# Weights 128 bytes away from the operands that stream past them

## The chip, the cores and the metric

The kernel runs on one core of a Trainium2 chip. The metric is device time in microseconds of one execution; where several runs are given, the median. Everything said of the hardware comes from the profile of one execution, taken by the hardware profiler: for each engine when an instruction started, how long it took and what it waited for. PE is TensorE (matmuls), PEld its loading of weights, DVE is VectorE, ACT ScalarE, POOL GpSimd; SP issues most of the DMA transfers.

## The reference

Two layers of an encoder block on 512 tokens of width 1024, all in float32:

```python
for l in range(DEPTH):
    x = x + 0.5 * swiglu_ffn(rmsnorm(x, ffn1_norm[l]), ffn1_w_in[l], ffn1_w_out[l])
    h = rmsnorm(x, mix_norm[l])
    u_rwkv, u_gla, u_xa, u_gate = split_cols(h @ w_in[l], (RWKV_COLS, GLA_COLS, XA_WIDTH, GATE_COLS))
    y_rwkv, v_first = rwkv7_mixer(u_rwkv, v_first, ...)
    y_gla = gla_mixer(u_gla, ...)
    y_xa = memory_attention(u_xa, rmsnorm(mem, mem_norm[l]), xa_w_kv[l])
    branches = jnp.stack([y_rwkv, y_gla, y_xa], axis=2)
    merged = jnp.einsum('bsjc,jcd,bsjd->bsd', branches, w_branch[l], jax.nn.sigmoid(gates))
    x = x + merged @ w_out[l]
    x = x + 0.5 * swiglu_ffn(rmsnorm(x, ffn2_norm[l]), ffn2_w_in[l], ffn2_w_out[l])
return rmsnorm(x, final_norm)
```

`swiglu_ffn` is `(silu(gate) * up) @ w_out` with a hidden width of 2816. Most of the work is matrix products with weights, in the four FFNs and in the projection `w_in` and the branches of the mixer.

## The kernel before

**Products in two halves.** A float32 operand is split into a rounded `hi` (ACT) and the rest `lo` (DVE, source minus `hi`), and a product is three matmuls: hi with hi, hi with lo, lo with hi. Activations are laid out with features on the partitions. In most products the weights are the stationary operand, 128 columns at a time, and the activations stream past them, 256 or 512 columns per matmul. In the row of a matmul, `ps_b<-xhi,hi` names the output, the streamed operand and the weights, in this order.

**Seven products instead of eight.** `seven` computes a product of 2x2 blocks by Winograd's scheme: seven parts, each a chain of 3n matmuls of 128x256 in `part` (n is 4, or 3 in the last block of the hidden width). The left factors are sums of quarters of the weights, made on DVE or by adding DMA transfers. They come as pieces, which `piece` splits into `hi` and `lo`:

- a *wide* piece holds the weights of two parts (`raw.shape[1] == 2`, 128x1024): `a` for the parts with `b11` and `n1`, `q` for `n2` and `b21`. Its halves stand in pool `wp` under the tags `whi` and `wlo`.
- a *narrow* piece holds those of one part (128x512): `e` twice, for `t3` and `b22`, and `d` for `t4`. Its halves stand in the pool of the stage (`ffn`, or `mg` in the mixer) under the tags `fhi` and `flo`, two buffers of each.

So a product has four parts on wide pieces and three on narrow ones. The right factors are made once: by `blocks_in` in pool `keep` (`xhi`, `xlo`, `n12`, `t3`) for the first FFN weight, and in the pool of the stage (`mh`, `ml`) for the second FFN weight and for the mixer's `w_out`. Tile `n12` shows in rows as `n`, `t3` as `t`.

**Where the work lies.** Each of the four FFNs has 22 hidden tiles. The first four are plain products of three matmuls of 128x512 on all of x (`whole`), the other 18 go through `seven`. After each block of 8, 8 and 6 hidden tiles, four calls of `seven` apply that block's rows of the second weight. In the mixer the projections are plain products with weights in `wp` (`wide`), 128x512 each, between many small float32 matmuls of the recurrences; the memory's keys are products of 128x256; `w_out` goes through `seven` four times per layer.

**Memory.** Pools are entered in the order `const`, `keep`, `wp`, `nrm`, and then those of the stage; tiles follow each other within a pool. A tile's start is rounded up to 32 bytes, so that each of the two `rt` buffers in `nrm`, 16 bytes long, takes 32; all other tiles of `keep`, `wp` and `nrm` are multiples of 256 bytes. `const` ends so that `keep` starts at 128 modulo 256. Hence the tiles of `keep`, `wp` and the `sq` tiles of `nrm` start at 128 modulo 256, those of `ffn` at 192.

**Order.** Every operation is first recorded; `plan` then simulates the engines with durations that depend on shapes only and issues each engine's queue in the order that the simulation finds. A tile's buffer is free for its next tile when all users of the old one are done (`gone`).

Of the kernel before, what the change touches and what calls it, by code (L numbers as in the profile page):

```python
# [11 lines left out]
F32 = mybir.dt.float32  # L12
F32R = mybir.dt.float32r
# [6 lines left out]
P = 128  # L20
T = 512
# [7 lines left out]
HALVES = slice(0, H), slice(H, T)  # L29
NWHOLE = [[4, 4], [4, 4]]  # L30
NWARM = 12
NQ = 5
EPS = 1e-6
LN_EPS = 64e-5
# [63 lines left out]
class Tile:  # L98
    def __init__(self, pool, shape, dt, name, tag, bufs):
        self.pool, self.shape, self.dt, self.name, self.tag, self.bufs = pool, shape, dt, name, tag, bufs  # L100
        self.real, self.users, self.writes, self.reads, self.runs = None, [], [], [], ([], [])
        self.before, self.gone, self.free = (), None, False
# [491 lines left out]
class Net:  # L594
    def __init__(self, ctx, tc, I):
        self.nc, self.I = Recorder(tc), I
        self.const = self.pool("const", 1)
        self.keep = self.pool("keep", 1)
        self.wp = self.pool("wp", 2)
        self.nrm = self.pool("nrm", 1)  # L600
        self.psb = self.pool("psb", 3, space=PSUM)
        self.pss = self.pool("pss", 1, space=PSUM)
        self.psy = self.pool("psy", 1, space=PSUM)
        self.dram = self.pool("dram", 1, space=bass.MemoryType.DRAM)
# [24 lines left out]
    def setup(self):  # L629
        nc, I = self.nc, self.I  # L630
        self.pars = [self.const.tile([P, NPAR], F32, name=f"par{l}", tag=f"par{l}") for l in range(L)]
        self.par = self.pars[0]
        nc.scalar.dma_start(out=self.par, in_=I["par"][0])
        self.one = self.const.tile([P, 1], F32, name="one", tag="one")
        nc.vector.memset(self.one, 1.0)
        ps = self.psy.tile([P, T], F32, name="ps_y", tag="y", free=True)
        for _ in range(NWARM):
            nc.tensor.matmul(ps[:, :P], self.one.to_broadcast([P, P]), self.one.to_broadcast([P, P]), start=True, stop=True)
        self.turn = 0
        self.xs = self.keep.tile([P, KD, T], F32, name="x", tag="x")  # L640
        self.x = [self.xs[:, k, :] for k in range(KD)]
        for k in range(KD):
            nc.sync.dma_start(out=self.x[k], in_=I["x"][k * P:(k + 1) * P, :])
        self.cst = self.const.tile([P, P], F32, name="cst", tag="cst")
        nc.sync.dma_start(out=self.cst, in_=I["cst"][:, :P])
        for l in range(1, L):
            nc.sync.dma_start(out=self.pars[l], in_=I["par"][l])
        self.eps = self.const.tile([P, 2], F32, name="eps", tag="eps")
        nc.vector.memset(self.eps[:, 0:1], EPS)
        nc.vector.memset(self.eps[:, 1:2], LN_EPS)  # L650

        self.sums, self.par7 = {}, False
        self.yd = self.dram.tile([3, P, T], F32, name="yd", tag="yd")
        self.yx = self.dram.tile([4, P, T], F32, name="yx", tag="yx")
        self.xd = self.dram.tile([KD, P, T], F32, name="xd", tag="xd")
        self.vd = [self.dram.tile([4, P, T], F32, name=f"vd{l}", tag=f"vd{l}") for l in range(L)]
# [127 lines left out]
    def raw_in(self, pool, norm):  # L784

        hi, lo = (pool.tile([P, 7, T], F32R, name="xr" + c, tag=f"m01{c}", bufs=1) for c in "hl")
        r = pool.tile([P, 2, T], F32R, name="xr", tag="q", bufs=NQ)
        xs = [(hi[:, k, :], lo[:, k, :]) for k in range(7)] + [(r[:, 0], r[:, 1])]
# [44 lines left out]

    def piece(self, pool, raw):

        p, tags = (self.wp, ("whi", "wlo")) if raw.shape[1] == 2 else (pool, ("fhi", "flo"))
        hi, lo = (p.tile(list(raw.shape), F32R, name=t[1:], tag=t, bufs=2) for t in tags)
        self.split(hi, lo, raw)
        return [(hi[:, c, :], lo[:, c, :]) for c in range(raw.shape[1])]

# [56 lines left out]
    def seven(self, pool, src, n, ops, evict, clear=False):  # L897
# [7 lines left out]
        def begin():  # L905
# [3 lines left out]
            nc.gpsimd.dma_start(out=a[:, 1], in_=w[:, 3], accum_op=ALU.add)  # L909
            q = ring("q", NQ)  # L910
            nc.sync.dma_start(out=q[:, 1], in_=w[:, 2])
            e = ring("q", NQ)
            nc.sync.dma_start(out=e[:, 0], in_=w[:, 1])
# [871 lines left out]
    def mem_norm(self, pool):  # L1785

        nc, I = self.nc, self.I
        mt = [pool.tile([P, 4, NMEM], F32, name="m", tag="q", bufs=NQ) for _ in range(2)]
        mt = [t[:, k, :] for t in mt for k in range(4)]
# [118 lines left out]
```

## Time and profile before

| | |
|---|---|
| median of 3 runs | 2533.76 us (2532.69 to 2534.31) |
| the profiled execution's own time | 2534.68 us |
| its span, first to last instruction | 2532.7 us |
| granted clock of TensorE | 0.999 |
| ACT busy | 1466.9 us, 58% of the span |
| POOL busy | 241.2 us, 10% |
| DMA | 358.02 MB, 141 GB/s in the mean |

The busy time of an engine is the union of its instructions. Matmuls overlap one another in their pipeline, so a row's duration is longer than the time from one start to the next; the latter, called pace below, is what a chain of matmuls costs. In a group's row stand the count, the busy time, the mean duration of one in ns, and the idle time before them with what ended it.

### The profile page before, as it was taken

To read this page: it belongs to the slowest core of one execution; us is meant where nothing else is said; L and a number is where in the kernel's file an instruction comes from. 1 tells how busy PE (TensorE), PEld (TensorE's weight loads), DVE (VectorE), ACT (ScalarE), POOL (GpSimd) and SP (SyncE) were. 2 spreads that over 40 slices of the span, in tenths; PEclk is the share of its full clock that TensorE was granted. 3 is DMA by queue.
4 is the path that set the end of the run, shared out by engine and by line. 5 is a ranking of instruction groups with operands and counts; after the bars stand their busy time and mean duration, and the time that the engine had idled before them with its cause. 6 is when DMAs were issued, how large, how long until landed. Compare 5 with 4: busy or idle time off the path is not lost.

```text
span 2532.7 us, 47197 instructions
## 1 busy us (share of the span) xinstructions
PE 2506.4 (99%) x17636; PEld 2270.3 (90%) x17636; DVE 2100.5 (83%) x4218; ACT 1466.9 (58%) x2660; POOL 241.2 (10%) x362
## 2 busy tenths in 40 slices
PE   9999999999999999999999999999999999999998
PEld 8999988888788799999989999887887888899998
DVE  8988885778888689888899888866888877898878
ACT  6665666564544456565665656664745444565655
POOL 1111100000000001111112111000000000011110
PEclk9999999999999999999999999999999999999999
DMA  7777762422222456877558777523222225468774
GB/s 199 194 197 189 165 190 76 125 73 69 70 83 74 141 159 150 204 186 184 143 143 203 187 184 170 176 88 101 84 72 88 67 77 171 134 162 205 188 180 105
DMA packets 163668, 358.02 MB, mean 141 GB/s; under 512 B 18256, under 2 KB 38160, under 8 KB 163440
## 3 DMA queue, kind: packets, MB, share of 16 engines
q1 hardware_dynamic: 125344, 288.87, 37.8%
q0 software_dynamic: 36864, 65.03, 16.2%
q8 instruction: 139, 2.28, 0.4%
q10 hardware_dynamic: 1232, 1.11, 0.1%
q14 instruction: 89, 0.73, 0.1%
HBM read 342.88 MB, written 12.06 MB: 140 GB/s over the span
## 4 chain that ended last, share of the span: by engine, by line
PE 85%; DVE 8%; DMA 3%; ACT 2%; issue 2%; SPq 0%; DVEq 0%; ACTq 0%; POOLq 0%
PE ps_b L316 40%; PE ps_i L316 25%; PE ps_f L316 10%; PE ps_c L316 9%; PE ps_y L316 1%; DVE wlo L316 1%; DVE lo L316 1%; DVE x L316 1%; DMA q<-in_ffn_out_dram 1%; ACT whi L316 1%; DMA wraw<-in_w_out_dram 0%; DVE ml L316 0%; DMA wraw<-in_ffn_in_dram 0%; ACT hi L316 0%; DMA q<-in_ffn_in_dram 0%
## 5 line engine op out<-in xcount | busy, mean ns | idle before, releaser
L316 ACT ACTIVATE hi<-q 128x512 fp32r<-128x512 f32 (+3 forms) x384 | 288.9, 756 | 204.8 <-PE ps_i L316 69.6
L316 DVE TENSOR_TENSOR lo<-q,hi 128x512 fp32r<-128x512 f32 (+3 forms) x384 | 321.6, 840 | 43.5 <-ACT hi L316 43.1
L316 PE MATMUL ps_b<-xhi,whi 128*128 128x512 f32 (+1 forms) x880 | 353.7, 402 | 0.2 <-DVE rk_r L316 0.2
L316 PE MATMUL ps_b<-xlo,whi 128*128 128x512 f32 (+1 forms) x880 | 352.9, 401 | 0.1
L316 PE MATMUL ps_b<-xhi,wlo 128*128 128x512 f32 x864 | 347.2, 402 | 0.6 <-DVE wlo L316 0.6
L316 DVE TENSOR_TENSOR wlo<-wraw,whi 128x1024 fp32r<-128x1024 f32 (+1 forms) x172 | 183.7, 1069 | 75.2 <-ACT whi L316 71.0
L316 ACT ACTIVATE whi<-wraw 128x1024 fp32r<-128x1024 f32 (+1 forms) x174 | 161.7, 929 | 130.0 <-PE ps_b L316 100.1
L316 DVE TENSOR_TENSOR lo<-wraw,hi 128x1024 fp32r<-128x1024 f32 (+2 forms) x162 | 191.5, 1182 | 48.5 <-ACT hi L316 46.5
L316 ACT ACTIVATE hi<-wraw 128x1024 fp32r<-128x1024 f32 (+2 forms) x162 | 166.3, 1026 | 106.1 <-PE ps_i L316 41.0
L316 PEld LDWEIGHTS ps_b<-xlo,whi 128*128 128x128 f32 (+1 forms) x880 | 164.1, 187 | 35.6 <-DVE xlo L316 2.5
L316 PEld LDWEIGHTS ps_b<-xhi,whi 128*128 128x128 f32 (+1 forms) x880 | 164.4, 187 | 33.6 <-issue 1.2
L316 PEld LDWEIGHTS ps_b<-xhi,wlo 128*128 128x128 f32 x864 | 162.7, 188 | 32.9 <-DVE wlo L316 2.4
L316 PE MATMUL ps_i<-mh,hi 128*128 128x256 f32 x628 | 157.1, 283 | 4.3 <-ACT hi L316 2.6
L316 PE MATMUL ps_i<-ml,hi 128*128 128x256 f32 x624 | 154.8, 281 | 0.0
L316 PE MATMUL ps_b<-xlo,hi 128*128 128x256 f32 x576 | 144.3, 283 | 0.0
L316 PE MATMUL ps_b<-xhi,hi 128*128 128x256 f32 x576 | 144.3, 283 | 0.0
L316 PEld LDWEIGHTS ps_i<-mh,hi 128*128 128x128 f32 x628 | 119.1, 190 | 5.9 <-ACT hi L316 3.2
L316 PEld LDWEIGHTS ps_i<-ml,hi 128*128 128x128 f32 x624 | 118.1, 190 | 0.0
L316 PEld LDWEIGHTS ps_b<-xhi,hi 128*128 128x128 f32 x576 | 110.5, 192 | 0.2
L316 PEld LDWEIGHTS ps_b<-xlo,hi 128*128 128x128 f32 x576 | 110.4, 192 | 0.2
L316 DVE TENSOR_TENSOR q<-q 128x512 f32<-128x512 f32 (+1 forms) x128 | 85.5, 668 | 22.9 <-DMA q<-in_ffn_in_dram 19.0
L316 ACT ACT_TABLE_LOAD x71 | 91.1, 1283 | 18.9 <-DVE gc L316 10.8
(416 smaller groups left out, 7021.4 us busy)
## 6 DMA issues: line engine op xcount, KB each, us to landing
wraw<-in_w_main_dram SPq DMA_DIRECT2D x108, 512.0 KB, 3.6
wraw<-in_ffn_in_dram SPq DMA_DIRECT2D x102, 512.0 KB, 4.6
q<-in_ffn_in_dram SPq DMA_DIRECT2D x144, 256.0 KB, 4.5
d<-in_ffn_in_dram SPq DMA_DIRECT2D x72, 256.0 KB, 4.2
q<-in_ffn_in_dram POOLq DMA_DIRECT2D x72, 256.0 KB, 6.0
wraw<-in_ffn_in_dram POOLq DMA_DIRECT2D x72, 256.0 KB, 5.2
wraw<-in_ffn_out_dram SPq DMA_DIRECT2D x32, 512.0 KB, 4.4
q<-in_ffn_out_dram SPq DMA_DIRECT2D x64, 256.0 KB, 3.7
```

The lines of the kernel that those rows point to most:

```text
L316: return getattr(getattr(self.tc.nc, engine), what)(*(f(v) for v in a), **{n: f(v) for n, v in k.items()})
```

## The change

Two pools with one unread tile each are put between the others: `shift`, 128 bytes, between `keep` and `wp`, and `level`, 64 bytes, behind `nrm`. The tiles are only cleared once on POOL. The two halves of a narrow piece, until now two tiles, become parts of one tile of 64 + 2 x 512 columns, in which `hi` starts at column 32 and `lo` 512 columns later.

```diff
+SHIFT = 32
...
         self.keep = self.pool("keep", 1)
+        self.shift = self.pool("shift", 1)
         self.wp = self.pool("wp", 2)
         self.nrm = self.pool("nrm", 1)
+        self.level = self.pool("level", 1)
...
+        nc.gpsimd.memset(self.shift.tile([P, SHIFT], F32, name="shift", tag="shift"), 0.0)
+        nc.gpsimd.memset(self.level.tile([P, 16], F32, name="level", tag="level"), 0.0)
...
     def piece(self, pool, raw):
 
-        p, tags = (self.wp, ("whi", "wlo")) if raw.shape[1] == 2 else (pool, ("fhi", "flo"))
-        hi, lo = (p.tile(list(raw.shape), F32R, name=t[1:], tag=t, bufs=2) for t in tags)
+        if raw.shape[1] == 2:
+            hi, lo = (self.wp.tile(list(raw.shape), F32R, name=t[1:], tag=t, bufs=2) for t in ("whi", "wlo"))
+        else:
+            n = raw.shape[2]
+            f = pool.tile([P, 64 + 2 * T], F32R, name="hl", tag="fhl", bufs=2)
+            hi, lo = (f[:, SHIFT + i * T:SHIFT + i * T + n].rearrange("p (c t) -> p c t", c=1) for i in range(2))
         self.split(hi, lo, raw)
```

Modulo 256, `wp` then starts at 0, `ffn` at 128, and the narrow halves at 0.

## The prediction

> **What bounds the kernel now.** I read the page first, then the waits of TensorE, the groups by shape, and a timeline of one product.
>
> ```profile
> PE 2506.4 (99%) x17636; PEld 2270.3 (90%) x17636; DVE 2100.5 (83%) x4218; ACT 1466.9 (58%) x2660; POOL 241.2 (10%) x362
> PE 85%; DVE 8%; DMA 3%; ACT 2%; issue 2%; SPq 0%; DVEq 0%; ACTq 0%; POOLq 0%
> ```
>
> ```profile
> PE ps_i L316 <- ACT hi L316: 2.6, 3, 1.2
> PE ps_b L316 <- DVE wlo L316: 2.0, 6, 0.6
> ```
>
> PE is busy 99% of the span and carries 85% of the chain that ended last; the two largest entries in its list of waits are 2.6 and 2.0 us. So PE starves almost nowhere. What remains is how fast one matmul follows another, and there the same shape has several speeds. In these timeline rows (start, duration, instruction) two chains of 12 matmuls, 128x256 each, run without a wait:
>
> ```profile
> 280.71 0.28 PE L316 MATMUL ps_b<-xhi,hi 128*128 128x256 f32 x1
> 280.71 0.19 PEld L316 LDWEIGHTS ps_b<-xlo,hi 128*128 128x128 f32 x1
> ...
> 282.15 1.11 PE L316 MATMUL ps_i<-t,hi 128*128 128x256 f32 x8
> ...
> 283.56 0.28 PE L316 MATMUL ps_b<-xhi,hi 128*128 128x256 f32 x1
> ```
>
> ```profile
> 245.17 0.28 PE L316 MATMUL ps_f<-mh,hi 128*128 128x256 f32 x1
> ...
> 246.53 0.28 PE L316 MATMUL ps_c<-mh,hi 128*128 128x256 f32 x1
> ```
>
> From 280.71 to 282.15: 1.44 us / 12 = **120 ns** a matmul. From 282.15 to 283.56: 1.41 / 12 = **117.5**. From 245.17 to 246.53: 1.36 / 12 = **113.3**. The second row shows why placement can matter: the weights of the next matmul are loaded from the moment at which the present one starts to stream, so both reads of SBUF run side by side.
>
> Where do these operands stand? Pools `keep` and `wp` follow each other and hold multiples of 256 bytes, so the streamed `xhi` and a wide piece in `whi` have the same address modulo 256: distance 0 (the 120). `nrm` ends with two `rt` buffers of 16 bytes in 32 each, so everything in `ffn` stands 64 further: the narrow piece that meets `t3` has distance 64 (the 117.5), and the streamed `mh` against a wide piece has 192 (the 113.3). The groups by shape say the same over the run (count, busy, mean ns):
>
> ```profile
> L316 PE MATMUL ps_i<-n,hi 128*128 128x256 f32 x576 | 80.9, 283 | 0.0
> L316 PE MATMUL ps_i<-t,hi 128*128 128x256 f32 x576 | 79.7, 281 | 0.6 <-ACT ft L316 0.6
> L316 PE MATMUL ps_b<-mh,hi 128*128 128x256 f32 x416 | 100.6, 278 | 0.0
> ```
>
> ```profile
> L316 PE MATMUL ps_f<-mh,hi 128*128 128x256 f32 x4 | 1.0, 276 | 0.0
> ```
>
> A duration is its pace plus about 163 ns (283 with 120; the last row, of the window 245 to 247 alone, has 276 with 113.3): `n` meets wide pieces only (distance 0), `t` narrow ones only (64), and `mh` into `ps_b` wide ones only (192), where 278 gives a mean pace of 115.
>
> **The change part by part.**
>
> *Distances.* `shift` (128 bytes) moves `wp` by 128 against `keep`; `level` (64) rounds the 128 + 64 up to 256, so `ffn` lines up with `keep`; inside it `hl` starts its narrow halves 128 bytes in. Every 256-wide product then has distance 128. From the code: 72 products of the first FFN weight have 48 matmuls on wide and 36 on narrow pieces; the four second weights 4 x 4 x 11 times 12 wide and 9 narrow; `w_out` 8 times 48 and 36; the memory's keys 192 wide. Distance 0: 3456 + 1584 + 288 + 192 = **5520**. Distance 64: **2592**. Distance 192: 2112 + 384 = **2496**.
>
> No 256-wide row shows distance 128. Bounds by the nearest: 120, no better than distance 0, or 113.3, as good as the best neighbour; below, a further step as large as the seen one, 106.7. Distance 0 is the worst, and both neighbours on the way to 128 are better, one reaching 113.3. I take **113.3**: 5520 x 6.7 = 37.0, 2592 x 4.2 = 10.9, 2496 x 1.7 = 4.2, together **52 us**.
>
> *The 512-wide matmuls* (about 3700) change distance too: projections from 0 to 128, the FFN's whole products from 192 to 128.
>
> ```profile
> 458.01 35.61 PE ps_b L316 x157
> ```
>
> ```profile
> L316 PE MATMUL ps_b<-xlo,whi 128*128 128x512 f32 x864 | 346.7, 401 | 0.0
> ```
>
> ```profile
> 8.12 0.39 PE L316 MATMUL ps_i<-xrh,lo 128*128 128x512 f32 x1
> ...
> 9.49 0.40 PE L316 MATMUL ps_i<-xrh,lo 128*128 128x512 f32 x1
> ```
>
> At distance 0 (the first two rows, a stretch of the chain and the group), 35.61 / 157 = 226.8 ns; at 192, 6 matmuls in 1.37 us = 228.3. Distance leaves no mark here, so I take **0**; bounds are a gain or a loss of 6.7 each, 25 us either way.
>
> *What is late next.* PE would ask for pieces 4% sooner. In the windows (busy us of PE, PEld, DVE, ACT, POOL; clock; DMA share; GB/s)
>
> ```profile
> 70.00:130.00 60.00, 57.94 (x483) 56.95 (x482) 57.61 (x116) 37.70 (x72) 9.52 (x11) 1.00 0.83 200
> 130.00:190.00 60.00, 60.00 (x506) 60.00 (x507) 51.50 (x94) 39.00 (x71) 12.11 (x14) 1.00 0.79 193
> 1000.00:1060.00 60.00, 60.00 (x512) 59.99 (x512) 57.49 (x111) 34.10 (x60) 11.21 (x13) 1.00 0.83 199
> 1320.00:1380.00 60.00, 60.00 (x509) 59.99 (x509) 59.86 (x117) 37.28 (x69) 10.36 (x12) 1.00 0.79 195
> 2250.00:2310.00 60.00, 60.00 (x510) 60.00 (x509) 58.02 (x114) 34.52 (x61) 11.81 (x14) 1.00 0.83 204
> ```
>
> DVE has 8.5 us to spare in 130 to 190, and the cover holds. In the first 60 us of each FFN it is busy 57.5 to 59.9 of 60, and in the first of them PE already loses 2.1. These four windows hold 483 + 512 + 509 + 510 = 2014 of the 10,608 matmuls, 10 us of the 52; I take three quarters of it, 7.5, as lost to DVE. Elsewhere transfers (share 0.79, then about 0.83) and buffers that come just in time cost some 2.5 more. Given back: **10**. If no cover held outside these windows either, half of the 52 would go.
>
> *One tile for hi and lo.* A narrow buffer now comes free after its `lo` matmuls, not its `hi` matmuls:
>
> ```profile
> 283.62 0.62 ACT L316 ACTIVATE hi<-d 128x512 fp32r<-128x512 f32 x1
> ...
> 287.63 0.63 ACT L316 ACTIVATE hi<-q 128x512 fp32r<-128x512 f32 x1
> ...
> 287.85 0.28 PE L316 MATMUL ps_i<-xhi,hi 128*128 128x256 f32 x1
> ...
> 288.39 0.69 DVE L316 TENSOR_TENSOR lo<-q,hi 128x512 fp32r<-128x512 f32 x1
> ...
> 288.80 0.64 PE L316 MATMUL ps_i<-xhi,lo 128*128 128x256 f32 x4
> ...
> 289.00 0.63 ACT L316 ACTIVATE hi<-q 128x512 fp32r<-128x512 f32 x1 [0.73 <-PE ps_i L316]
> ```
>
> ```profile
> 292.15 1.11 PE L316 MATMUL ps_i<-t,hi 128*128 128x256 f32 x8
> ```
>
> ACT at 289.00 waited for the last `hi` matmul of the piece begun at 287.85; it would wait for the four `lo` ones, until about 289.45, 4 x 0.12 = 0.48 us later. Queued behind it on ACT are the `ft` and `mh` steps of the hidden tile, which PE needs only in the block's second products, and on DVE the `lo` subtraction follows `hi`. The piece written at 283.62 is first used at 287.85, the one of 287.63 at 292.15: over 4 us of lead against 0.63 + 0.69 + 0.48. Cost **0**; without that lead, 0.48 for each of 3 x 128 narrow pieces. Whether a matmul on `hi` would wait for the write of `lo` in the same tile is answered by a row:
>
> ```profile
> 9.47 0.71 ACT L316 ACTIVATE xrh<-x,par 128x512 fp32r<-128x512 f32 x1
> ```
>
> `xrh` is one tile of seven slices, and ACT writes one while matmuls on others (8.12, 9.49) run: waits go by region.
>
> *The rest.* Two memsets on POOL, at most about 241.2 / 362 = 0.67 us each by the page's mean, which nobody reads: 0. No DMA is added or moved past a queue; all land in shifted tiles. The planner knows neither address nor pace; only the later release can alter its order, which I put at 0, plus or minus 5 us.
>
> **Sum:** 52 - 10 = 42 us. The profiled execution took 2534.68 us for a span of 2532.7, and lies 0.9 above the median of 2533.76. 2534.68 - 42 - 0.9 gives **2492 us** beside the median.
>
> [...]
>
> **The rivals.**
>
> 1. *Still better than any neighbour.* At 128 the two reads never meet, and the pace falls as far again, to 106.7: 10,608 x 6.7 = 71 more, 123 in all. DVE's 51.5 us of work would then nearly fill the 54 us left of such a window, so I keep some 70%: 2534 - 86 = **2448**. Against: every 120, 117.5 and 113.3 above is a settled pace, and nothing is below the last.
> 2. *Nothing.* The paces depend on the order of wide and narrow pieces, not on addresses, or the stages that matter are held by DVE: **2534**. Against: `n` and `t` pieces differ within one product.
> 3. *128 acts like 64.* All at 117.5: 5520 x 2.5 - 2496 x 2.5 = 8 us: **2526**.
> 4. *Slower: 128 is a second meeting point.* The streams move at different speeds, so a distance of half a period may only shift the collision to mid-stream. At 120 for all, distance 64 loses 2592 x 2.5 = 6.5 and 192 loses 2496 x 5 = 12.5: **2553**. It decides from a pace of 118.2, the mean now. For it: 64 and 192 aren't alike, so the place of the minimum isn't shown.
> 5. *Slower by the shared tile.* If a tenth of the 384 releases reached PE, 18 us come off the gain; all of it is eaten at a quarter: about **2540** beyond that.
>
> **How the numbers follow.** Forecast 0.50 (its own range 2478 to 2508, from the give-back and the order); rival 1 0.16; rival 2 0.08; rival 3 0.15; rival 4 0.08; rival 5 0.03. The range 2446 to 2532 leaves out rivals 4 and 5, much of 2, and the far side of 1; the 512-wide bounds of 25 us lie inside it. By 0.2%, 5 us, about what a measurement of this kernel can tell: faster 0.50 + 0.16 + 0.11 of rival 3 = 0.77; same 0.08 + 0.04 = 0.12; slower 0.11.
>
> **What would show it.** Right: `n`, `t` and `mh` groups all at about 276 ns with no wide or narrow difference; some 525 to 530 matmuls in a 60 us window of the later FFN instead of 506; DVE near full from the start of each FFN; 512-wide groups unchanged at 401. Wrong: durations that stay mixed (rival 2), 281 everywhere (rival 3), 283 (rival 4), under 272 (rival 1), or idle time of PE at narrow pieces ended by ACT `hi` or DVE `lo` (rival 5). The give-back is wrong if PE's idle total, now 2532.7 - 2506.4 = 26 us, doesn't grow.

## The result, and the profile after

The changed kernel took **2546.26 us** (median of 5 runs, 2544.37 to 2551.26) against 2533.0 before on the same chip: a ratio of **1.0054, 95% interval 1.0041 to 1.0066**. It is slower by 13 us, where a gain of 42 was forecast, and lies 14 us above the range.

The page of the changed kernel, its span, engines and chain:

```profile
span 2545.3 us, 47187 instructions
...
PE 2524.9 (99%) x17636; PEld 2282.1 (90%) x17636; DVE 2105.5 (83%) x4218; ACT 1475.4 (58%) x2660; POOL 242.0 (10%) x364
...
PE 88%; DVE 7%; DMA 2%; ACT 1%; issue 1%; SPq 0%; DVEq 0%; POOL 0%; POOLq 0%; ACTq 0%
```

The profiled execution took 2547.34 us of its own. PE has the same 17636 matmuls and is busy 18.5 us longer (2524.9 against 2506.4), while its idle time fell from 26 to 2545.3 - 2524.9 = 20 us. So no new wait made the kernel slower: the matmuls themselves follow one another more slowly. The groups by shape (count, busy, mean ns of one, idle before):

```profile
L317 PE MATMUL ps_b<-xlo,whi 128*128 128x512 f32 x864 | 348.8, 404 | 0.0
...
L317 PE MATMUL ps_i<-t,hl 128*128 128x256 f32 x864 | 114.6, 282 | 0.0
...
L317 PE MATMUL ps_b<-mh,hi 128*128 128x256 f32 x416 | 103.0, 282 | 0.0
...
L317 PE MATMUL ps_i<-n,hi 128*128 128x256 f32 x576 | 80.5, 282 | 0.0
```

`n`, `t` and `mh` are now alike, as the forecast wanted, but at 282 ns, not at 276: `n` won 1 ns, `t` lost 1, `mh` lost 4. And the 512-wide group went from 401 to 404. A timeline of one stretch in which the pace has settled, that is, repeats from part to part (start, duration, instruction):

```profile
252.36 0.28 PE L317 MATMUL ps_b<-xhi,hi 128*128 128x256 f32 x1
...
253.80 1.12 PE L317 MATMUL ps_c<-n,hi 128*128 128x256 f32 x8
...
255.24 0.28 PE L317 MATMUL ps_f<-mh,hl 128*128 128x256 f32 x1
```

Each of the two parts takes 1.44 us for 12 matmuls, 120 ns. The stretch of the projections in the chain of work that ended last had 35.61 us for 157 matmuls before, 226.8 ns each; now it has

```profile
457.64 36.48 PE ps_b L317 x157
```

which is 232.4 ns each. And the windows (busy us of PE, PEld, DVE, ACT, POOL; clock; DMA share; GB/s) show 503 to 508 matmuls in the settled ones where 525 to 530 were forecast, at the same clock:

```profile
130.00:190.00 60.00, 60.00 (x508) 60.00 (x507) 51.56 (x95) 41.35 (x76) 11.27 (x13) 1.00 0.77 189
...
1320.00:1380.00 60.00, 60.00 (x503) 60.00 (x501) 59.74 (x115) 38.88 (x72) 10.38 (x12) 1.00 0.76 183
```

**The sum by distance.** For the rest of this text every matmul on `hi` and `lo` tiles (their type is float32r) was put beside its operands' addresses in the compiled program. Its *distance* is the start of the next matmul's weights minus the start of its own streamed operand, modulo 256; its *pace* is the time to the next start, of which anything above 125 ns (256-wide) or 242 ns (512-wide) is counted as a wait and not as pace.

| matmuls | before: count, mean pace | after: count, mean pace |
|---|---|---|
| 256-wide, distance 0 | 5593 at 119.7 ns | |
| 256-wide, 64 | 2587 at 117.4 | |
| 256-wide, 192 | 2513 at 115.4 | |
| 256-wide, 128 | | 10,623 at 119.1 |
| 512-wide, 0 | 2903 at 230.7 | |
| 512-wide, 192 | 783 at 229.5 | |
| 512-wide, 128 | | 3683 at 233.3 |

256-wide: 5593 x 0.6 = 3 us won, 2587 x 1.7 = 4 and 2513 x 3.7 = 9 lost, together 10 lost. 512-wide: 2903 x 2.6 + 783 x 3.8 = 10 lost. Waits at 256-wide matmuls fell by 5 and all else by 2.7. But for rounding, that makes the 12.6 us by which the two spans differ. It doesn't say yet that distance causes it, or whether 128 could ever have had the 113.3.

### The profile page after: what moved, and what is told of

It is laid out like the page before. It is cut to its first block, busy times and chain, and to the rows that moved or that the text cites. A ratio compares the mean times of both kernels' runs of the same rounds, so it can differ in the third digit from the quotient of the medians.

```text
span 2545.3 us, 47187 instructions
## 1 busy us (share of the span) xinstructions
PE 2524.9 (99%) x17636; PEld 2282.1 (90%) x17636; DVE 2105.5 (83%) x4218; ACT 1475.4 (58%) x2660; POOL 242.0 (10%) x364
## 3 DMA queue, kind: packets, MB, share of 16 engines
q8 instruction: 139, 2.28, 0.4%
## 4 chain that ended last, share of the span: by engine, by line
PE 88%; DVE 7%; DMA 2%; ACT 1%; issue 1%; SPq 0%; DVEq 0%; POOL 0%; POOLq 0%; ACTq 0%
PE ps_b L317 42%; PE ps_i L317 26%; PE ps_f L317 10%; PE ps_c L317 9%; PE ps_y L317 1%; DVE wlo L317 1%; DMA wraw<-in_ffn_in_dram 1%; DVE x L317 1%; DMA q<-in_w_out_dram 0%; ACT whi L317 0%; DMA q<-in_ffn_in_dram 0%; DMA q<-in_ffn_out_dram 0%; DVE S L317 0%; DVE lo L317 0%; DVE t L317 0%
## 5 line engine op out<-in xcount | busy, mean ns | idle before, releaser
L317 ACT ACTIVATE hl<-q 128x512 fp32r<-128x512 f32 (+1 forms) x256 | 158.3, 619 | 142.5 <-PE ps_i L317 45.7
L317 DVE TENSOR_TENSOR hl<-q,hl 128x512 fp32r<-128x512 f32 (+1 forms) x256 | 171.5, 671 | 11.1 <-ACT hl L317 10.0
L317 ACT ACTIVATE hi<-q 128x1024 fp32r<-128x1024 f32 (+1 forms) x128 | 132.1, 1032 | 79.8 <-PE ps_b L317 60.1
L317 DVE TENSOR_TENSOR lo<-q,hi 128x1024 fp32r<-128x1024 f32 (+1 forms) x128 | 152.3, 1190 | 28.1 <-ACT hi L317 27.5
L317 PE MATMUL ps_i<-mh,hl 128*128 128x256 f32 x832 | 167.8, 283 | 1.2 <-DVE x L317 0.9
L317 PEld LDWEIGHTS ps_i<-mh,hl 128*128 128x128 f32 x832 | 135.8, 189 | 1.8 <-issue 1.2
L317 ACT ACTIVATE hl<-d 128x512 fp32r<-128x512 f32 (+1 forms) x128 | 79.1, 618 | 64.8 <-PE ps_i L317 38.8
L317 PE MATMUL ps_i<-xhi,hl 128*128 128x256 f32 x576 | 114.6, 282 | 0.0
L317 PE MATMUL ps_i<-t,hl 128*128 128x256 f32 x864 | 114.6, 282 | 0.0
```

The costliest lines, as they stand in the source:

```text
L317: return getattr(getattr(self.tc.nc, engine), what)(*(f(v) for v in a), **{n: f(v) for n, v in k.items()})
```

## The experiments

Every ratio is to the kernel before on the same chip, with its 95% interval. All times are medians of 4 to 11 runs; the paces and shares are those of one profiled execution each, which took 2529.39 us in `d64` and 2513.61 in `m192_0`, above their medians.

### One distance for everything

The changed kernel with another distance: the sizes of the unread tiles and the start of the narrow halves. Nothing else differs, and the order of wide and narrow pieces stays. `d0` is

```diff
-SHIFT = 32
+SHIFT = 0
...
-        nc.gpsimd.memset(self.shift.tile([P, SHIFT], F32, name="shift", tag="shift"), 0.0)
-        nc.gpsimd.memset(self.level.tile([P, 16], F32, name="level", tag="level"), 0.0)
+        nc.gpsimd.memset(self.level.tile([P, 48], F32, name="level", tag="level"), 0.0)
```

> The changed kernel with every distance (start of the weights minus start of the streamed operand, modulo 256) set to 0 instead of 128; the shared narrow tile stays. Theory A (the pace of matmuls depends on the distance, and 128 is a poor one): the 256-wide pace goes to the 119.7 ns that distance 0 had in the kernel before, the 512-wide to 230.5, so 10,600 x 0.6 = 6 us are lost and 3700 x 2.5 = 9 us won against the changed kernel's 2546: 2543. Theory B (the 13 us come from the shared tile and the order it brings): 2546 as changed, since the tile stays. Theory C (absolute places count, not distances): no forecast, any pace.

`d64` and `d192` (here `d64`; `d192` has 48 in `SHIFT` and `shift`, and no tile in `level`):

```diff
-SHIFT = 32
+SHIFT = 16
...
+        nc.gpsimd.memset(self.shift.tile([P, 16], F32, name="shift", tag="shift"), 0.0)
+        nc.gpsimd.memset(self.level.tile([P, 32], F32, name="level", tag="level"), 0.0)
```

> The changed kernel with every distance set to 64. A: 256-wide pace 117.4 ns as at distance 64 before, so 10,600 x 1.7 = 18 us less than 2546; 512-wide 231 by 31 rows of before, 3700 x 2 = 7 less: 2521. B: 2546. C: no forecast.

> The changed kernel with every distance set to 192. A: 256-wide pace 115.4 ns as at distance 192 before (113.3 if the fast state is kept throughout), so 10,600 x 3.7 = 39 us less than 2546, 512-wide 229.4, 3700 x 3.6 = 13 less, and some 10 us given back to DVE: about 2500, faster than the kernel before. B: 2546. C: no forecast.

`d128_moved` keeps distance 128 and moves all pools from `keep` on by 64 bytes:

```diff
+        self.base = self.pool("base", 1)
         self.keep = self.pool("keep", 1)
...
+        nc.gpsimd.memset(self.base.tile([P, 16], F32, name="base", tag="base"), 0.0)
```

> The changed kernel, distance 128 kept, with all of its pools moved by 64 bytes. A: paces and time as changed, 119.1 and 233.0 ns, 2546 within 3 us. B: the same. C: another pace, and a time that differs by more than 5 us.

As these four showed a pace that isn't monotone, the steps between were run too: `d32`, `d96`, `d160` and `d224`, with 8, 24, 40 and 56 as `SHIFT`.

> Every distance 32. Measured so far with all distances alike: 0 gives settled paces of 120 ns, 64 gives 117.7 and 113.3, 192 gives 117.7 (113.3 rarely), 128 gives 120 and 118.7. Theory D (0 and 128 are special, every other distance has the same two settled paces, and chance gaps pick one): 113.3 and 117.7, mean 116 to 117.7, time 2524 to 2530. Theory S (the pace changes smoothly with distance): between 0 and 64, about 118, time 2533.

> Every distance 96. D: 113.3 and 117.7, mean 116 to 117.7, 2524 to 2530. S: between 64 and 128, about 117.6 to 118.5, time 2530 to 2538.

> Every distance 160. D: 113.3 and 117.7, mean 116 to 117.7, 2524 to 2530. S: between 128 and 192, about 118.4, time 2537.

> Every distance 224. D: 113.3 and 117.7, mean 116 to 117.7, 2524 to 2530. S: between 192 and 0, about 118.9, time 2535.

| distance | kernel | median us | ratio | 256-wide mean pace | 512-wide mean pace |
|---|---|---|---|---|---|
| 0 | d0 | 2544.24 | 1.0044 [1.0029, 1.0058] | 120.0 | 230.1 |
| 32 | d32 | 2541.27 | 1.0034 [1.0021, 1.0047] | 118.4 | 233.8 |
| 64 | d64 | 2524.46 | 0.9967 [0.9956, 0.9978] | 116.1 | 234.0 |
| 96 | d96 | 2542.59 | 1.0041 [1.0026, 1.0056] | 118.4 | 234.6 |
| 128 | changed kernel | 2546.26 | 1.0054 [1.0041, 1.0066] | 119.1 | 233.3 |
| 128 | d128_moved | 2548.34 | 1.0061 [1.0046, 1.0076] | 119.3 | 233.4 |
| 160 | d160 | 2556.82 | 1.0096 [1.0081, 1.0111] | 120.0 | 234.3 |
| 192 | d192 | 2526.45 | 0.9978 [0.9968, 0.9987] | 117.7 | 230.8 |
| 224 | d224 | 2529.41 | 0.9986 [0.9977, 0.9996] | 117.2 | 233.9 |

Where the narrow piece of `t` and the wide one of `n` had different paces before, all have one at distance 0. Groups and a stretch of the chain of `d0`:

```profile
L317 PE MATMUL ps_i<-t,hl 128*128 128x256 f32 x864 | 115.4, 283 | 0.0
...
L317 PE MATMUL ps_i<-n,hi 128*128 128x256 f32 x576 | 81.1, 283 | 0.0
```

```profile
457.81 35.59 PE ps_b L317 x157
```

`t` went from 281 to 283 by its address alone, and the projections run at 35.59 / 157 = 226.7 ns again. In `d64` the same stretch has

```profile
452.00 36.64 PE ps_b L317 x157
```

233.4 ns, and its FFN runs in places at 113.3 (timeline):

```profile
192.30 1.07 PE L317 MATMUL ps_c<-n,hi 128*128 128x256 f32 x8
...
193.66 0.28 PE L317 MATMUL ps_f<-xhi,hl 128*128 128x256 f32 x1
...
195.02 0.28 PE L317 MATMUL ps_i<-xhi,hl 128*128 128x256 f32 x1
...
196.47 0.74 PE L317 MATMUL ps_i<-xhi,hl 128*128 128x256 f32 x4 [0.38 <-DVE hl L317]
197.04 1.07 PE L317 MATMUL ps_i<-n,hi 128*128 128x256 f32 x8
...
198.40 0.28 PE L317 MATMUL ps_b<-xhi,hi 128*128 128x256 f32 x1
```

192.30 to 193.66 and 193.66 to 195.02 are 1.36 us for 12, and the part behind the 0.38 us of waiting again takes 198.40 - 197.04 = 1.36. What follows:

- **Distance sets the mean pace; the place didn't where it was tried, at 128.** One program with other addresses takes from 2524.5 to 2556.8 us, and moving everything by 64 bytes at an unchanged distance moves the paces by 0.2 ns and the time by 2 us, with overlapping intervals. The times that theory A gave came out at 0 and nearly at 64 (2543 and 2521), but not at 192: there 115.4 ns and about 2500 us were expected, and 117.7 ns and 2526 came.
- **The pace isn't smooth in the distance, and 128 isn't a special point either.** Both theories fall: S expected 2537 us at 160, which took 2557 and is the slowest of all, and D expected at most 2530 at 32, 96 and 160, and fits 224 alone. 64, with 116.1 ns, lies far below its neighbours 32 and 96 with 118.4 each.
- **The 512-wide matmuls have an order of their own:** 0 and 192 are the best two with 230.1 and 230.8 ns, everything else costs 2.5 to 4.5 ns more.

At 160 even matmuls on one set of weights differ. Groups of `d160`:

```profile
L317 PE MATMUL ps_b<-xlo,hi 128*128 128x256 f32 x576 | 144.4, 284 | 0.0
L317 PE MATMUL ps_b<-xhi,hi 128*128 128x256 f32 x576 | 143.9, 279 | 0.0
```

What streams isn't the reason. The single paces go round in sixes, 116, 125, 116, 124, 118, 121 in one stretch, with a mean of 120.0, and `xhi` and `xlo` fall on alternate places; in the last four matmuls of these parts, where `xhi` alone streams, the means still go 117, 124, 116, 123. In the changed kernel the paces likewise go round 122, 118, 120 in many stretches.

### The shared tile alone

`shared_only` is the kernel before with the two halves of a narrow piece in one tile, without the added pools, so that all distances are those of before:

```diff
+SHIFT = 0
...
+            f = pool.tile([P, 2 * T], F32R, name="hl", tag="fhl", bufs=2)
+            hi, lo = (f[:, SHIFT + i * T:SHIFT + i * T + n].rearrange("p (c t) -> p c t", c=1) for i in range(2))
```

> The kernel before with only the shared narrow tile of the change (hi and lo in one tile, no column offset, no shift or level pool), so that every distance is as before. Theory A (distances carry the 13 us): 2533 within 4 us, 256-wide paces 119.7, 117.4 and 115.4 at distances 0, 64 and 192 as before. Theory B (the shared tile's later release and the order it brings carry them): 2540 to 2546.

It took 2530.85 us, ratio **1.0001 [0.9992, 1.001]**. Paces are 119.7, 117.4 and 115.1 at 0, 64 and 192, those of before within 0.3 ns. The later release costs nothing that can be measured.

### Mixed distances

The 512-wide matmuls had their lowest mean pace at distance 0 (230.1 ns, `d0`), the 256-wide ones at 64 (116.1, `d64`). Both can be had in one kernel: the wide halves stand in two persistent tiles with two turns each, the narrow ones in one such tile of the stage, and each use chooses where in its turn it starts (`PLAIN` for 512-wide, `WIDE` for wide pieces, `E0`, `E1` and `D0` for the three narrow ones, in units of 4 bytes). `m64` has 64 bytes for every piece:

```diff
-SHIFT = 32
+PLAIN, WIDE, E0, E1, D0 = 0, 16, 16, 16, 16
...
+        self.halves = [self.wp.tile([P, 64 + 4 * T], F32R, name=t, tag=t, bufs=1) for t in ("whi", "wlo")]
...
+        hi, lo = self.halves_at(PLAIN, raw.shape[1])
...
-            self.part(Y, self.piece(pool, e[:, 0:1])[0], ops["t3"], False)
+            self.part(Y, self.piece(pool, e[:, 0:1], E0)[0], ops["t3"], False)
```

> Distance 64 for all 256-wide products of seven, 0 for all 512-wide ones (two fixed tiles with turns taken by hand make room for it). Pace by distance alone: 116.1 ns for the 256-wide as in the run with all distances 64 (2524.5), 230.1 for the 512-wide as with all distances 0: 3600 x 3.9 = 14 us less than 2524.5, so 2510. If the 512-wide pace isn't a matter of distance: 2524.

`m192_0` puts the pieces at 192, except the first narrow one, which meets `t3`, at 0. It asks whether the 113.3 seen at 192 before came from the distance or from the distance-0 stretch ahead of it:

```diff
-PLAIN, WIDE, E0, E1, D0 = 0, 16, 16, 16, 16
+PLAIN, WIDE, E0, E1, D0 = 0, 48, 0, 48, 48
```

> As the last, but the 256-wide products at distance 192, except the first narrow piece of each product of seven, which stands at 0; 512-wide at 0. Theory H (where a distance has two settled paces, the stretch before picks one; 192 entered from a stretch at 0 settles at 113.3, as in the kernel before): mean pace (120 + 6 x 113.3) / 7 = 114.3 against 118.1 before, 10,600 x 3.8 = 40 us, some 10 given back to DVE: about 2500. Rival (chance gaps alone pick the pace, which for 192 was 117.7 in the run with all distances 192): (120 + 6 x 117.7) / 7 = 118.0, about 2527.

`m192` then takes that one stretch away again (`E0` is 48), and `m128_0` and `m64_0` do at 128 and at 64 what `m192_0` does at 192 (`0, 32, 0, 32, 32` and `0, 16, 0, 16, 16`):

> This is m192_0 with one number changed: the first narrow piece of each product, the one that meets t3 and that stood at distance 0 there (1769 of the 256-wide matmuls), now stands at distance 192 like all other 256-wide weights; the 512-wide stay at distance 0. Theory H (at distance 192 two settled paces exist, 113.3 and 117.7 ns, and a stretch at distance 0 just before picks the faster one): with that stretch gone most 256-wide matmuls settle at 117.7, as in d192 (97% there). Against m192_0 that is 8921 x 3.5 = +31 us, less 1769 x 1.7 = 3 us and some 10 us of waits that go when PE is slower: about 2522 to 2532 us, slower than m192_0 by more than 10. Theory N (m192_0 was faster than d192 because its 512-wide weights stand at 0, or because its halves lie in persistent tiles, and 192 is simply a good distance): nearly all settle at 113.3, and the 1769 gain some 5.2 ns each: 2511.9 - 9 = about 2503 us. A mix of paces with a time between 2508 and 2520 would speak for neither.

> m192_0 with 128 in the place of 192: the first narrow piece of each product stays at distance 0 (1769 matmuls of 256), all other 256-wide weights stand at distance 128 (8921), the 512-wide at 0. Theory P (128 is a poor distance in itself and has no fast state): the 8921 run at the 119.1 ns that they have in the changed kernel; the 512-wide save 3716 x 3.2 = 12 us against the changed kernel: 2546 - 12 = about 2534 us (2528 to 2540). Theory E (the forecast's 113.3 was within reach, and the change lost it because it took every distance-0 stretch away with which the fast state is entered): most of the 8921 settle at 113.3 or near it: 8921 x 5 = 45 us less, with 10 given back in waits about 2500 us (2493 to 2510).

> The same with 64: 1769 matmuls at distance 0, 8921 at 64, the 512-wide at 0. Its neighbour is m64 (all 256-wide at 64: 2524.16 us, 117.7 ns in 83% and 113.3 in 15%). Theory H (a distance-0 stretch just before picks the faster of the two settled paces, at 64 as at 192): most settle at 113.3, mean about 114.2: 8921 x 2.9 = 26 us less than m64, 1769 x 2.3 = 4 more, waits some 10 more: about 2512 us (2505 to 2517), as m192_0. Theory H192 (the entry works at 192 alone): the 8921 stay at 117.1, the 1769 cost 4 us: about 2528 us.

| kernel | 256-wide at | median us | ratio | of these at 113 or 114 ns | their mean pace |
|---|---|---|---|---|---|
| m64 | 64 | 2524.16 | 0.9969 [0.9956, 0.9981] | 16% | 117.1 |
| m64_0 | 64, first narrow at 0 | 2529.46 | 0.9992 [0.9983, 1.0001] | 4% | 117.6 |
| m192 | 192 | 2528.01 | 0.9987 [0.9978, 0.9996] | 2% | 117.8 |
| **m192_0** | 192, first narrow at 0 | **2511.86** | **0.9912 [0.9898, 0.9926]** | 83% | 114.2 |
| m128_0 | 128, first narrow at 0 | 2534.54 | 1.0013 [1.0004, 1.0022] | 1% | 118.7 |

(Percentages and means are of the 10,409 matmuls at 64 or 192 in `m64` and `m192`, and of the 8921 at the main distance in the others; the 1769 at distance 0 have 119.3 to 119.8.) In all five the 512-wide mean is 230.0 or 230.1.

`m192_0` against `m192` is the pair that matters. Timeline of one product of `m192_0` (wide pieces are named `whi` in these kernels):

```profile
193.52 1.60 PE L317 MATMUL ps_i<-t,hl 128*128 128x256 f32 x12
194.96 0.28 PE L317 MATMUL ps_b<-xhi,whi 128*128 128x256 f32 x1
...
196.32 1.07 PE L317 MATMUL ps_c<-n,whi 128*128 128x256 f32 x8
...
197.68 0.28 PE L317 MATMUL ps_f<-xhi,hl 128*128 128x256 f32 x1
```

and the same parts of `m192`:

```profile
193.92 1.57 PE L317 MATMUL ps_i<-t,hl 128*128 128x256 f32 x12
195.33 0.28 PE L317 MATMUL ps_b<-xhi,whi 128*128 128x256 f32 x1
...
196.75 1.10 PE L317 MATMUL ps_c<-n,whi 128*128 128x256 f32 x8
...
198.16 0.28 PE L317 MATMUL ps_f<-xhi,hl 128*128 128x256 f32 x1
```

`t` takes 1.44 us in the first (distance 0, 120 ns) and 1.41 in the second (192, 117.5). The two parts behind it stand at 192 in both kernels, and take 1.36 us each in the first (113.3) and 1.42 and 1.41 in the second. **At distance 192 there are two settled paces, and a part at distance 0 ahead of it picks the faster one** (113.3 against 117.5 ns): in `m192_0`, with its 1769 slower matmuls at distance 0, 83% of the 8921 at 192 run at 113 or 114 ns, in `m192`, without them, 2% of 10,409. Over the whole traces, the part behind `t` runs at the faster pace in 71 of 72 cases in `m192_0`, and in none of 72 in `m192`, `m64_0` and `m128_0` each. The time of `m192_0` lies between those of its two theories (about 2500 and 2527); the paces decide for H.

At 64 the same entry picks nothing faster, 117.5 ns behind it (timeline of `m64_0`, where `t` stands at 0):

```profile
192.67 1.60 PE L317 MATMUL ps_i<-t,hl 128*128 128x256 f32 x12
194.11 0.28 PE L317 MATMUL ps_b<-xhi,whi 128*128 128x256 f32 x1
...
195.52 1.11 PE L317 MATMUL ps_c<-n,whi 128*128 128x256 f32 x8
```

`t` has 120, and the part behind it 1.41 us, 117.5. The theory that a stretch at distance 0 picks the faster pace wherever there are two is wrong: of the distances tried with that entry it works at 192 alone. What picks 113.3 at 64, in 40% of the matmuls of `d64` and in 16% of `m64`, isn't shown, but the traces show where it is picked: at waits. Of the changes between a stretch of at least five matmuls at 112 to 115 ns and one at 116 to 119, all 31 in `m64` and 26 of 33 in `d64` stand at a start that came over 125 ns after the last, and the pace behind such a wait may be either. At 192 waits lose the faster pace: 28 of the 29 direct drops to the slower one in `m192_0` stand at one. The smaller share of 113.3 ate the gain of `m64`, for which 2510 us had been expected: the 512-wide matmuls won 3716 x 4.0 = 15 us against `d64`, the 256-wide lost 10,409 x 1.0 = 10, and the medians are 0.3 us apart.

`m128_0` came out at the time (2534) that its expectation gives if 128 is poor in itself. Its timeline, with `t` at 0:

```profile
191.79 1.36 PE L317 MATMUL ps_i<-t,hl 128*128 128x256 f32 x10
192.98 0.28 PE L317 MATMUL ps_b<-xhi,whi 128*128 128x256 f32 x1
...
194.40 1.11 PE L317 MATMUL ps_c<-n,whi 128*128 128x256 f32 x8
...
195.83 0.28 PE L317 MATMUL ps_f<-xhi,hl 128*128 128x256 f32 x1
```

The two parts behind `t` take 1.42 and 1.43 us, 118 and 119 ns: it has the entry and keeps a mean of 118.7.

What a faster PE runs into is seen in `m192_0`, in the page, the waits of TensorE (total us, times, longest) and two windows:

```profile
PE 2477.4 (99%) x17636; PEld 2239.6 (89%) x17636; DVE 2091.5 (83%) x4218; ACT 1459.8 (58%) x2658; POOL 241.5 (10%) x363
```

```profile
PE ps_i L317 <- ACT ft L317: 4.2, 4, 1.6
PE ps_b L317 <- ACT whi L317: 2.7, 3, 0.9
PE ps_i L317 <- ACT hl L317: 2.4, 2, 1.8
```

```profile
70.00:130.00 60.00, 57.32 (x486) 56.17 (x485) 57.76 (x117) 37.12 (x72) 10.35 (x12) 1.00 0.81 203
130.00:190.00 60.00, 58.33 (x499) 57.74 (x498) 49.74 (x92) 38.70 (x71) 10.38 (x12) 1.00 0.79 191
190.00:250.00 60.00, 60.00 (x524) 59.93 (x523) 53.29 (x99) 35.02 (x61) 11.22 (x13) 1.00 0.79 189
```

The span is 2511.2 us, so PE idles for 2511.2 - 2477.4 = 34 us, 8 more than before. The paces themselves won 33 us of 256-wide time (1263 us before, by the first table, against 1769 x 119.4 + 8921 x 114.2 = 1230); 256-wide waits took 13.5 back, and 20 are left. The third window has 524 matmuls, just under the 525 to 530 of the forecast; the first two lose 2.7 and 1.7 us of PE. ACT heads the list of waits, but it was held up itself: of the four longest waits of PE in these two windows, two are for an `ft` before which ACT had waited 2.28 and 1.17 us for DVE, and two for an `hl` before which ACT had waited 2.01 and 1.44 us for a DMA of `q`.

## Why the prediction was wrong

- **What bounds the kernel: right.** PE's pace decides. `d160` (slowest) and `m192_0` (fastest) differ by 45 us with the same 17636 matmuls, at a PE share of 99% each.
- **That the distance causes the paces: right,** and now shown, by one program at eight distances and by the move at an equal distance. With the order of wide and narrow pieces unchanged, which the second rival took for the cause, the mean pace of the 128x256 matmuls goes from 116.1 (`d64`) to 120.0 ns (`d0`, `d160`) by the addresses alone, and with the mixed distances down to 114.2 (`m192_0`, its main distance).
- **The step that failed: 113.3 for a distance that no row showed.** "Distance 0 is the worst, and both neighbours on the way to 128 are better" took the better of the three paces that were seen, at 0, 64 and 192, for that of the distance between them. The runs have 118.4 at 96, 119.1 at 128 and 120.0 at 160. And the 113.3 wasn't the pace of distance 192: it is one of two there, and before it was mostly entered from distance-0 stretches: in the trace before, 61 of the 75 passages from a slower stretch to one at 112 to 115 ns come directly from one at 120. The prediction had the hint in its own row, where `mh` at 278 "gives a mean pace of 115". Making all distances alike takes such entries away as well, but `m128_0` shows that the lack of such an entry isn't what cost the 113.3 at 128: with the entry, the mean there is 118.7. The term of 52 us won measured 10 lost.
- **The 512-wide matmuls: wrong, within the bound.** "Distance leaves no mark here" rested on the rows of 0 and 192, which are the two best of eight. Put at 0, it measured 10 us lost, of the 25 allowed either way.
- **What is late next: in the changed kernel not tested,** since PE became slower; its idle time fell by 6 us. Where PE did become faster, in `m192_0`, the mechanism shows as described, in the first windows of the FFN, but it was sized too small: 13.5 of 33 us given back, where 10 of 52 were taken. Behind ACT, which heads the list of waits, stood DVE, as the forecast had it, and as often a DMA; how much of the 13.5 us is whose wasn't separated.
- **The shared tile at 0: right** (`shared_only`, 1.0001).
- **The memsets at 0** weren't tried apart; `d64` carries both and `d192` one, and both kernels are faster than before.
- **The rivals.** The fourth came nearest, with the sign and 7 us beside the time: its break-even pace of 118.2 fits the kernel before, with 118.1, and a changed kernel that has 119.1 and is slower. But its mechanism, a second meeting point at half the period, isn't borne out: the 256-wide pace at 160 is as bad as at 0 (120.0 each), and nothing sets 128 with its 119.1 apart from its neighbours 96 and 160 (118.4 and 120.0). The bounds of 113.3 and 120 held for the mean pace at every distance; the range failed because it gave the upper one too small a chance.

What stays open is the mechanism beneath: why these distances have these paces, why 192 has two, and which way a wait at 64 will turn it. No run here looks inside the reads. That the period is 256 bytes wasn't tried apart either; it fits `d0`, where distances of many different multiples of 256 nearly all have 120 ns.

## What to carry to other kernels

Where matmuls follow each other without waits, the addresses of weights and streamed operand against each other are worth measuring, at every step and for each width by itself: here 32 us lay between the best and the worst single distance (`d64` and `d160`), and the best version, `m192_0` with 2511.86 us, mixes them. A pace seen in these traces belongs to its distance and, at 192, to what ran just ahead of it (113.3 ns behind a part at distance 0 in `m192_0`, 117.5 without one in `m192`), so a value for a distance that was never run should carry the whole span of the seen paces, not the better end. An edit that makes everything uniform also takes away whatever the mixture did: between `m192_0` and `m192` that was 16 us.

## What was not expected of the hardware

- Mean paces of 128x256 float32r matmuls with a new weight load each, in one profiled execution of `d0`, `d32`, `d64`, `d96`, the changed kernel, `d160`, `d192` and `d224`, that is, by distance modulo 256 in steps of 32: 120.0, 118.4, 116.1, 118.4, 119.1, 120.0, 117.7, 117.2 ns; of 128x512: 230.1, 233.8, 234.0, 234.6, 233.3, 234.3, 230.8, 233.9.
- Two settled paces at one distance: at 192, 1.36 us for 12 matmuls in `m192_0` (113.3 ns) and 1.41 to 1.42 in `m192` (117.5 to 118.3). In `m192_0` 28 of the 29 direct drops from the faster to the slower one stand at a wait, and in `d64` 113.3 came back at once behind a wait of 0.38 us. In `d224` there are two as well, near 116.5 and 118 over 12 successive matmuls.
- The lowest settled pace in the timelines of 128x256 matmuls is 113.3 ns (before, `d64` and `m192_0`: 1.36 us for 12). Of the four stretches of 157 projections, 128x512 with a weight load each, `d0` has the lowest pace with 226.7 ns (before 226.8, changed kernel 232.4, `d64` 233.4).
